# Square root on ACT and one Newton step for the reciprocal roots of the MLP and final norms, and POOL's squares of the second token half issued later

## The chip, the cores and the metric

The kernel runs on one core of one Trainium2 chip. The metric is the device time of one execution in microseconds (us), as the median of several executions. The core has five engines with instruction queues of their own: PE (matrix multiply), DVE (vector), ACT (scalar, functions from tables), POOL (a second elementwise engine) and SP (which issues DMAs). Each engine works its queue in order, and they wait for each other through semaphores.

## The reference, cut to what matters

A trunk of two layers on 1024 tokens of width 1024, in float32. Each layer mixes tokens (a gated MLP, a state space block and attention, side by side), then adds a squared-ReLU MLP; a last RMSNorm ends it. The change concerns three of the norms: that ahead of the MLP, in each of the two layers, and the last one.

```python
def rmsnorm(x, g):
    xf = x.astype(jnp.float32)
    var = jnp.mean(xf * xf, axis=-1, keepdims=True)
    return (xf * lax.rsqrt(var + EPS)).astype(x.dtype) * g
...
def squared_relu_mlp(h, w1, w2):
    return jnp.square(jax.nn.relu(h @ w1)) @ w2
...
        x = x + mix @ w_out[l]
        x = x + squared_relu_mlp(rmsnorm(x, norm_mlp_g[l]), mlp_w1[l], mlp_w2[l])
    return rmsnorm(x, final_norm_g)
```

## The kernel before, in words

Activations lie feature-major: `xt` is eight tiles of 128 features by 1024 tokens, and "half n" is 512 of the tokens. Each matrix product is done in three passes of a high and a low part (`whi`, `wlo`, `bhi`, `blo`), which ACT and DVE make (`split`: ACT casts, DVE subtracts). The products from `w_out` on are blocked as a seven-product scheme: a class `Run` walks through stages (`w_out`, then four times `w1` and `w2`), each of fourteen steps of 24 matmuls into `st` (line L998 in the profile). A stage's products are numbered p = 1 to 7, each in two steps (kh = 0 and 1). `hooks` maps (stage, step) to work that is put in behind that step.

A norm half goes like this. `after_mix` or `finish` squares each tile half on ACT (`sq<-x`) and adds the squares: the first four tiles on POOL, the others on DVE. `sq_rstd` lets PE sum over the features with eight small matmuls into `pss` (the tokens then lie on partitions, 128x4), and `rstd` forms the reciprocal root on DVE: the sum plus epsilon (`rv`), a first guess from the float's bits (`ry`, two integer operations), and three Newton steps of three operations (`rt`, `rt`, `ry`), twelve small operations in a row. PE then spreads `ry` over the partitions (`rb<-cs,ry`, eight small matmuls in the trace), ACT copies `rb` out of PSUM, and DVE forms the normed half `hB` (eight operations), which is split again for the next stage. In the last norm (`close_r`, `close_x`) the products go to `out` instead.

There are six such halves: in each layer half 0, whose `norm_r` and `norm_x` stand behind steps 10 and 11 of stage 0, and half 1, behind steps 0 and 1 of stage 1; and at the end half 1 (behind steps 10 and 11 of stage 8) and half 0 (`finish`, behind the last step). I call them A0 and B0 in layer 0, A1 and B1 in layer 1, and F and the tail. `rstd` serves other norms too (tags "n" and those of the attention), which the change leaves alone.

The order on each engine is not the order of the code: the tile framework schedules the instructions by a model of the engines, and `tc.high_priority()` lifts what is inside it ahead of other work. `L.zo` and `z_evac` belong to the start of layer 1: ACT empties the projection tiles `zps` with a Tanh, a copy and a small copy `dk`, and so frees their PSUM banks for later `zps` matmuls.

Of the kernel before, what the change touches and what calls it, by code (L numbers as in the profile page):

```python
# [9 lines left out]
F32 = mybir.dt.float32  # L10
F32R = mybir.dt.float32r
I32 = mybir.dt.int32
AF = mybir.ActivationFunctionType
ALU = mybir.AluOpType
# [4 lines left out]
P = 128  # L19
# [3 lines left out]
KD = D // P  # L23
DEPTH = 2
EPS = 1e-6
# [42 lines left out]
def trunk(ctx, tc, x, w_zdk, w_uv, w_f, w_q, w_kv, w_out, w1, w2, gains, pcol, prow, w_s, cst, out):  # L68
    nc = tc.nc

    const = ctx.enter_context(tc.tile_pool(name="const", bufs=1))
    rawp = ctx.enter_context(tc.tile_pool(name="raw", bufs=RAW))
    bigp = ctx.enter_context(tc.tile_pool(name="big", bufs=2))
    small = ctx.enter_context(tc.tile_pool(name="small", bufs=4))
# [4 lines left out]
    def G(dt=F32, name="g"):  # L79
        return gp.tile([P, 1024], dt, tag="g", name=name)  # L80

    def BIG(dt, name="big"):
        return bigp.tile([P, 8192], dt, tag="big", name=name)
# [3 lines left out]
    def bank(tag, name):  # L87
        return ps.tile([P, 512], F32, tag=tag, name=name, bufs=BANKS[tag])
# [5 lines left out]
    act = nc.scalar  # L94
    dve = nc.vector
    pool = nc.gpsimd
    pe = nc.tensor

    def tt(o, a, b, op, eng=None):
        (eng or dve).tensor_tensor(out=o, in0=a, in1=b, op=op)  # L100

    def stt(o, a, s, b, op0, op1):
        dve.scalar_tensor_tensor(out=o, in0=a, scalar=s, in1=b, op0=op0, op1=op1)

    def ts(o, a, s1, op0, s2=None, op1=None, eng=None):
        if op1 is None:
            (eng or dve).tensor_scalar(out=o, in0=a, scalar1=s1, scalar2=None, op0=op0)  # L107
        else:
            (eng or dve).tensor_scalar(out=o, in0=a, scalar1=s1, scalar2=s2, op0=op0, op1=op1)
# [8 lines left out]
    def mm(o, l, r, start, stop):  # L118
        pe.matmul(o, lhsT=l, rhs=r, start=start, stop=stop)  # L119

    def rstd(ss, n, tag):
        v = small.tile([P, n], F32, tag=tag + "v", name="rv")
        ts(v, ss, EPS, ALU.add)
        y = small.tile([P, n], F32, tag=tag + "y", name="ry")
        yi = y.bitcast(I32)
        ts(yi, v.bitcast(I32), 1, ALU.logical_shift_right)
        ts(yi, yi, -1, ALU.mult, MAGIC, ALU.add)
        t = small.tile([P, n], F32, tag=tag + "t", name="rt")
        for _ in range(3):
            tt(t, y, y, ALU.mult)  # L130
            stt(t, t, -0.5, v, ALU.mult, ALU.mult)
            stt(y, t, 1.5, y, ALU.add, ALU.mult)
        return y
# [12 lines left out]
    ones = const.tile([P, P], F32, name="ones")  # L146
    dve.memset(ones, 1.0)
    act.copy(maskq_r, ones)
    warm = bank("c", "warm")
    for _ in range(WARM):  # L150
        mm(warm[:, 0:P], ones, ones, True, True)
# [99 lines left out]
    def sq_rstd(acc, tag, t0=0, t1=NT, tg="c"):  # L251
        n = t1 - t0
        pss = bank(tg, "pss")
        for t in range(t0, t1):
            for i, q in enumerate(acc):
                mm(pss[:, t * 2:t * 2 + 2], q[:, t * P:(t + 1) * P], ones[:, 0:2], i == 0, i == len(acc) - 1)
        acc.clear()
        return rstd(pss[:, 2 * t0:2 * t1:2], n, tag)

    def hsl(h, k, a, b):  # L260
        return h[:, k * S + a:k * S + b]
# [55 lines left out]
    def z_rest(L):  # L317
        L.yb = [G(F32, "yb") for _ in range(3)]
        for n in range(4, NT):
            z_tile(L, n, PA("zps"))  # L320
            if n == 4:
                L.r = sq_rstd(L.sq, "n")
                ts(L.rh, L.r, 0.5, ALU.mult)
            if n == 5:
                for i in range(4):
                    z_evac(L, L.zo[i], L.zt[i])
            if n > 5:
                z_evac(L, L.zo[n - 2], L.zt[n - 2])
            if n == 5:
                prefetch(taken[0] + 2)  # L330
        for n in range(NT - 2, NT):
            z_evac(L, L.zo[n], L.zt[n])
        L.zo = L.wz = None
# [206 lines left out]
    def ssd_norm(L):  # L540
        yr = rstd(L.yss.rearrange("p c g -> p (c g)"), 16, "y").rearrange("p (c g) -> p c g", g=2)
        for j, segs in enumerate((((0, 128, 0),), ((0, 64, 0), (64, 128, 1)), ((0, 128, 1),))):
            v = L.yb[j].rearrange("p (c d) -> p c d", c=NT)
            for a, b, gq in segs:
                tt(v[:, :, a:b], v[:, :, a:b], yr[:, :, gq:gq + 1].broadcast_to([P, NT, b - a]), ALU.mult)

    def gmlp(L):
        vr = rstd(L.vss, NT, "v")
        for j in range(2):
            v = L.vv[j].rearrange("p (c d) -> p c d", c=NT)  # L550
            tt(v, v, vr.unsqueeze(2).broadcast_to([P, NT, P]), ALU.mult)
            tt(v, v, L.vg[:, j * P:(j + 1) * P].unsqueeze(1).broadcast_to([P, NT, P]), ALU.mult)
# [175 lines left out]
    def attention(L, l, xsrc):  # L728
# [140 lines left out]
        for _ in mixing:  # L869
            pass  # L870
        R = mlp(L, l, xsrc)
        R.prep(1)
        drain(2, VKEEP)
# [24 lines left out]
    def half(n):  # L898
        return slice(n * 512, n * 512 + 512)
# [150 lines left out]
    def sq_half(acc, xm, m, n, eng=None):  # L1050
        if m == 0 and acc:
            act.activation(acc[0][:, half(n)], xm[:, half(n)], AF.Square, scale=1.0 / 32.0)
            return
        sq = G(F32, "sq")
        act.activation(sq[:, half(n)], xm[:, half(n)], AF.Square, scale=1.0 / 32.0)  # L1055
        if m == 0:
            acc.append(sq)
        else:
            tt(acc[0][:, half(n)], acc[0][:, half(n)], sq[:, half(n)], ALU.add, eng)

    def half_bcast(r, o):
        for t in range(4):
            mm(o[:, t * P:(t + 1) * P], r[:, t:t + 1].broadcast_to([P, P]), ident, True, True)

    def mlp(L, l, xsrc):
# [3 lines left out]
        xt = [G(F32, "x") for _ in range(KD)]  # L1069
# [3 lines left out]
        acc, rs = {}, {}  # L1073
# [7 lines left out]
            return [mix[b * 4 + kh * 2 + kk][:, half(n)] for kk in range(2)]  # L1081

        def norm_r(n):
            rs[n] = sq_rstd(acc[n], "m", n * 4, n * 4 + 4, "a")

        def norm_x(n):
            if not hB:
                scr.clear()
                hB.append(BIG(F32, "hB").rearrange("p (k t) -> p k t", k=KD))
            o = bank("a", "rb")  # L1090
            half_bcast(rs.pop(n), o)
            rb = G(F32, "rb")
            act.copy(rb[:, 0:512], o)
            for m in range(KD):
                stt(hB[0][:, m, half(n)], xt[m][:, half(n)], gcol[:, 2 * l + 1, m:m + 1], rb[:, 0:512], ALU.mult, ALU.mult)

        def after_mix(p):
            if p == 3:
                acc[0] = []
                for m in range(4):  # L1100
                    sq_half(acc[0], xt[m], m, 0, pool)
            elif p == 7:
                for m in range(4, KD):
                    sq_half(acc[0], xt[m], m, 0)
            elif p == 2:
                acc[1] = []
                for m in range(4):
                    sq_half(acc[1], xt[m], m, 1, pool)
            elif p == 4:
                mix.clear()  # L1110
                for m in range(4, KD):
                    sq_half(acc[1], xt[m], m, 1)

        def to_next(p):
            if p == 2:
# [37 lines left out]
        def close_r(n):  # L1153
            rs[n] = sq_rstd(acc[n], "f", n * 4, n * 4 + 4, "a")
# [25 lines left out]
        class LazyB:  # L1180
            def __getitem__(self, k):
                return hB[0][k]

        stages = [Stage(w_out[l], mix_half, LATE1, add_to(xt, True, False, after_mix), True, False, scratch)]
        for q in range(NQ):
            end = q == NQ - 1
            stages.append(Stage(w1[l, q], halves_of(LazyB()), EARLY1 if q == 0 else LATE1, relu_to(Lazy())))
            stages.append(Stage(w2[l, q], halves_of(Lazy()), LATE1,
                                add_to(xt, False, not end, (finish if last else to_next) if end else None), chain=not end))
        hooks = {(0, 10): [lambda: norm_r(0)], (0, 11): [lambda: norm_x(0)],  # L1190
                 (1, 0): [lambda: norm_r(1)], (1, 1): [lambda: norm_x(1)]}
        if last:
            hooks[8, 10] = [lambda: close_r(1)]
            hooks[8, 11] = [lambda: close_x(1, 0)]
# [159 lines left out]
```

## Time and profile before

| | us |
|---|---|
| median of 3 runs (lowest, highest) | 2228.8 (2227.22, 2229.75) |
| the profiled execution, its own time | 2227.68 |
| its span, first to last instruction | 2225.8 |
| PE busy (share of the span) | 2180.0 (98%) |
| DVE busy | 1669.2 (75%) |
| ACT busy | 1131.5 (51%) |
| POOL busy | 470.9 (21%) |
| granted TensorE clock, mean | 0.992 |

The times are of single executions, the engine rows of one profiled execution; its time lies 1.1 us under the median. A share of busy time says how full an engine is, not how much shorter the kernel would be without a piece of its work: that is read at the place where the engine that sets the end waits. The granted clock is a share of TensorE's full 2.4 GHz; 0.5 is its lower level, 1.2 GHz.

### The profile page before, as it was taken

To read this page: it belongs to the slowest core of one execution; us is meant where nothing else is said; L and a number is where in the kernel's file an instruction comes from. 1 tells how busy PE (TensorE), PEld (TensorE's weight loads), DVE (VectorE), ACT (ScalarE), POOL (GpSimd) and SP (SyncE) were. 2 spreads that over 40 slices of the span, in tenths; PEclk is the share of its full clock that TensorE was granted. 3 is DMA by queue.
4 is the path that set the end of the run, shared out by engine and by line. 5 is a ranking of instruction groups with operands and counts; after the bars stand their busy time and mean duration, and the time that the engine had idled before them with its cause. 6 is when DMAs were issued, how large, how long until landed. Compare 5 with 4: busy or idle time off the path is not lost.

```text
span 2225.8 us, 28714 instructions
## 1 busy us (share of the span) xinstructions
PE 2180.0 (98%) x10844; PEld 1854.6 (83%) x10844; DVE 1669.2 (75%) x2516; ACT 1131.5 (51%) x1841; POOL 470.9 (21%) x444
## 2 busy tenths in 40 slices
PE   9999999999999999999999999999899999999996
PEld 8888989877888888888898888988788888888885
DVE  6788688788775876767847868878888767677576
ACT  6363577545445445355534626774464453543543
POOL 3152266121010001001301613751110010001011
PEclk9999999999999999999999999999999999999998
DMA  5211301354555546535412112023565465456532
GB/s 182 65 53 57 86 1 71 82 132 102 126 132 136 122 104 144 147 90 121 154 49 69 60 45 67 1 98 74 123 153 122 104 142 142 105 109 147 131 67 76
DMA packets 63625, 222.15 MB, mean 100 GB/s; under 512 B 7456, under 2 KB 7552, under 8 KB 63488
## 3 DMA queue, kind: packets, MB, share of 16 engines
q0 software_dynamic: 20736, 75.51, 19.6%
q1 hardware_dynamic: 42752, 144.83, 19.6%
q8 instruction: 85, 1.39, 0.2%
q14 instruction: 52, 0.43, 0.1%
HBM read 211.87 MB, written 8.44 MB: 99 GB/s over the span
## 4 chain that ended last, share of the span: by engine, by line
PE 94%; DVE 2%; issue 2%; ACT 1%; DMA 0%; POOL 0%; POOLq 0%; SPq 0%; ACTq 0%; DVEq 0%
PE st L998 61%; PE cqkv L119 5%; PE xbc L119 5%; PE uvps L119 4%; PE av L119 4%; PE sc L119 3%; PE zps L119 2%; PE pTp L789 2%; PE qps L119 2%; PE yps L119 1%; PE vps L119 1%; PE knps L119 1%; PE rb L119 1%; DVE mx L751 1%; DMA x<-in_x 0%
## 5 line engine op out<-in xcount | busy, mean ns | idle before, releaser
L998 PE MATMUL st<-blo,whi 128*128 128x512 f32 x2016 | 787.2, 390 | 0.0
L998 PE MATMUL st<-bhi,wlo 128*128 128x512 f32 x2016 | 786.6, 390 | 0.0
L998 PE MATMUL st<-bhi,whi 128*128 128x512 f32 x2016 | 781.4, 391 | 2.4 <-ACT bhi L115 2.4
L998 PEld LDWEIGHTS st<-bhi,whi 128*128 128x128 f32 x2016 | 380.5, 189 | 81.3 <-ACT bhi L115 2.7
L998 PEld LDWEIGHTS st<-bhi,wlo 128*128 128x128 f32 x2016 | 380.2, 189 | 79.1
L998 PEld LDWEIGHTS st<-blo,whi 128*128 128x128 f32 x2016 | 380.5, 189 | 78.3
L192 POOL DMA_DIRECT2D ssum<-in_w x96 | 84.2, 883 | 923.8 <-DVE wlo L100 380.5
L100 DVE TENSOR_TENSOR wlo<-raw,whi 128x1024 fp32r<-128x1024 f32 (+3 forms) x188 | 239.0, 1272 | 53.9 <-issue 29.8
L100 DVE TENSOR_TENSOR x<-x,st 128x512 f32<-128x512 f32 x296 | 196.0, 680 | 32.9 <-PE st L998 32.5
L115 ACT CAST bhi<-tsum 128x1024 fp32r<-128x1024 f32 x96 | 101.0, 1052 | 215.0 <-DVE tsum L100 173.9
L115 ACT CAST whi<-raw 128x1024 fp32r<-128x1024 f32 (+3 forms) x188 | 193.8, 1034 | 16.2 <-DVE blo L100 12.7
L107 POOL TENSOR_SCALAR p<-p,sm 128x1024 f32<-128x1024 f32 (+6 forms) x84 | 158.9, 1901 | 113.7 <-DVE sm L774 81.8
L115 ACT CAST whi<-ssum 128x1024 fp32r<-128x1024 f32 x108 | 113.5, 1051 | 112.2 <-PE st L998 57.1
L100 DVE TENSOR_TENSOR wlo<-ssum,whi 128x1024 fp32r<-128x1024 f32 x108 | 131.8, 1220 | 49.7 <-ACT whi L115 27.6
L100 DVE TENSOR_TENSOR blo<-tsum,bhi 128x1024 fp32r<-128x1024 f32 x96 | 117.3, 1222 | 46.4 <-ACT bhi L115 46.0
L119 PE MATMUL av<-pT,vhi 128*128 128x256 f32 x480 | 113.5, 298 | 0.8 <-DVE pT L100 0.5
L1043 ACT ACTIVATE hid<-hid 128x1024 f32<-128x1024 f32 x64 | 67.9, 1061 | 84.3 <-DVE hid L1036 84.0
L1036 DVE CUSTOM_DVE_ANT_0 hid<-st,hid 128x512 f32<-128x512 f32 x96 | 65.2, 686 | 56.8 <-PE st L998 56.5
L119 PE MATMUL sc<-B 96*128 96x384 f32 (+11 forms) x432 | 101.0, 351 | 3.1 <-ACT p L764 1.8
L100 POOL TENSOR_TENSOR sq<-sq 128x512 f32<-128x512 f32 (+1 forms) x37 | 60.7, 1647 | 191.9 <-ACT sq L1055 179.9
L100 DVE TENSOR_TENSOR blo<-hB,bhi 128x1024 fp32r<-128x1024 f32 x48 | 58.7, 1223 | 48.5 <-ACT bhi L115 48.5
L764 ACT ACTIVATE p<-sc,mx 128x512 f32<-128x512 f32 (+3 forms) x144 | 83.2, 583 | 21.0 <-DVE mx L100 14.2
(244 smaller groups left out, 3647.2 us busy)
## 6 DMA issues: line engine op xcount, KB each, us to landing
raw<-in_w SPq DMA_DIRECT2D x128, 512.0 KB, 3.7
ssum<-in_w POOLq DMA_DIRECT2D x96, 512.0 KB, 5.7
ssum<-in_w SPq DMA_DIRECT2D x32, 512.0 KB, 4.5
raw<-in_w POOLq DMA_DIRECT2D x32, 512.0 KB, 9.3
raw<-in_w_f SPq DMA_DIRECT2D x20, 512.0 KB, 3.5
x<-in_x SPq DMA_DIRECT2D x16, 512.0 KB, 6.9
raw<-in_w_out SPq DMA_DIRECT2D x16, 512.0 KB, 3.7
dec<-adr SPq DMA_DIRECT2D x16, 384.0 KB, 3.5
```

Source lines behind the costliest of these rows:

```text
L100: (eng or dve).tensor_tensor(out=o, in0=a, in1=b, op=op)
L107: (eng or dve).tensor_scalar(out=o, in0=a, scalar1=s1, scalar2=None, op0=op0)
L115: act.copy(hi, src)
L119: pe.matmul(o, lhsT=l, rhs=r, start=start, stop=stop)
L192: pool.dma_start(out=o, in_=src, accum_op=ALU.add)
L751: dve.reduce_max(mx[:, n:n + 1], on, axis=AX.X, negate=True)
L764: act.activation(pw[:, n * wh:(n + 1) * wh], os[n][:, :wh], AF.Exp, bias=mx[:, 0:1], accum_out=sm[:, n:n + 1])
L789: pe.transpose(pt[:, c0:c0 + P], pp[j][:, kt * P:(kt + 1) * P], ident)
L998: pe.matmul(os[j], lhsT=w[:, cw], rhs=b[:, cb], start=first and n == 0, stop=last and n == 2, skip_group_check=True)
L1036: dve._custom_dve(TENSOR_ADD_SAT, out=d, in0=os[j], in1=d, s0=0.0 if full[0] else BIGGEST, s1=-BIGGEST if full[0] else 0.0)
L1043: act.activation(d, d, AF.Square)
```

## The change

`sq_rstd` calls a new function for the tags "m" (the norm ahead of the MLP) and "f" (the last norm). It takes the square root on ACT with epsilon as a bias tile, the reciprocal on DVE, and one Newton step instead of three. `norm_r`, the broadcast of `norm_x`, and the squares of tiles 4 to 7 are put under `tc.high_priority()`. The squares of tiles 0 to 3 of half 1, with POOL's additions, leave `after_mix` (p = 2) and go behind step 12 of stage 0, after `norm_x(0)`. In `finish` the squares stay where they were.

```diff
+    def rstd_act(ss, n, tag):
+        v = small.tile([P, n], F32, tag=tag + "v", name="rv")
+        y = small.tile([P, n], F32, tag=tag + "y", name="ry")
+        t = small.tile([P, n], F32, tag=tag + "t", name="rt")
+        act.activation(t, ss, AF.Sqrt, bias=eps)
+        ts(v, ss, EPS, ALU.add)
+        dve.reciprocal(y, t)
+        tt(t, y, y, ALU.mult)
+        stt(t, t, -0.5, v, ALU.mult, ALU.mult)
+        stt(y, t, 1.5, y, ALU.add, ALU.mult)
+        return y
...
+    eps = const.tile([P, 1], F32, name="eps")
+    dve.memset(eps, EPS)
...
-        return rstd(pss[:, 2 * t0:2 * t1:2], n, tag)
+        return (rstd_act if tag in ("m", "f") else rstd)(pss[:, 2 * t0:2 * t1:2], n, tag)
...
         def norm_r(n):
-            rs[n] = sq_rstd(acc[n], "m", n * 4, n * 4 + 4, "a")
+            with tc.high_priority():
+                rs[n] = sq_rstd(acc[n], "m", n * 4, n * 4 + 4, "a")
...
-            o = bank("a", "rb")
-            half_bcast(rs.pop(n), o)
-            rb = G(F32, "rb")
-            act.copy(rb[:, 0:512], o)
+            with tc.high_priority():
+                o = bank("a", "rb")
+                half_bcast(rs.pop(n), o)
+                rb = G(F32, "rb")
+                act.copy(rb[:, 0:512], o)
...
             elif p == 7:
-                for m in range(4, KD):
-                    sq_half(acc[0], xt[m], m, 0)
-            elif p == 2:
-                acc[1] = []
-                for m in range(4):
-                    sq_half(acc[1], xt[m], m, 1, pool)
+                with tc.high_priority():
+                    for m in range(4, KD):
+                        sq_half(acc[0], xt[m], m, 0)
             elif p == 4:
                 mix.clear()
-                for m in range(4, KD):
-                    sq_half(acc[1], xt[m], m, 1)
+                with tc.high_priority():
+                    for m in range(4, KD):
+                        sq_half(acc[1], xt[m], m, 1)
+
+        def squares():
+            acc[1] = []
+            for m in range(4):
+                sq_half(acc[1], xt[m], m, 1, pool)
...
+                 (0, 12): [squares], (1, 0): [lambda: norm_r(1)], (1, 1): [lambda: norm_x(1)]}
```

What the scheduler makes of it, at three places of layer 0. On DVE at A0, from the sum of the squares on, before the change (`x<-x,st` adds the products of the step that ends here to `xt`; one more Newton operation pair and `hB` x8 follow):

```order
L107 TENSOR_SCALAR rv<-pss 128x4
L100 TENSOR_TENSOR x<-x,st 128x512
L107 TENSOR_SCALAR ry<-rv 128x4
L109 TENSOR_SCALAR ry<-ry 128x4
L100 TENSOR_TENSOR rt<-ry 128x4
L100 TENSOR_TENSOR x<-x,st 128x512
L103 SCALAR_TENSOR_TENSOR rt<-rt,rv 128x4
L103 SCALAR_TENSOR_TENSOR ry<-rt,ry 128x4
L100 TENSOR_TENSOR rt<-ry 128x4
L103 SCALAR_TENSOR_TENSOR rt<-rt,rv 128x4
L103 SCALAR_TENSOR_TENSOR ry<-rt,ry 128x4
L100 TENSOR_TENSOR rt<-ry 128x4
```

The same place with the change:

```order
L107 TENSOR_SCALAR rv<-pss 128x4
L127 RECIPROCAL ry<-rt 128x4
L100 TENSOR_TENSOR x<-x,st 128x512
L100 TENSOR_TENSOR rt<-ry 128x4
L103 SCALAR_TENSOR_TENSOR rt<-rt,rv 128x4
L103 SCALAR_TENSOR_TENSOR ry<-rt,ry 128x4
L100 TENSOR_TENSOR x<-x,st 128x512
L103 SCALAR_TENSOR_TENSOR hB<-x,gcol,rb 128x512 x8
```

Twelve small operations have become five, and only one of the two additions to `x` is left between them. In the built program `rv` and, through it, the reciprocal wait for ACT's square root.

On ACT at A0 before the change, from the casts ahead of it to the casts for stage 1:

```order
L115 CAST bhi<-scr 128x1024
L1055 ACTIVATE sq<-x 128x512 x4
L1093 COPY rb<-rb 128x512
L115 CAST whi<-raw 128x1024
L115 CAST bhi<-hB 128x1024
L115 CAST whi<-raw 128x1024
L115 CAST bhi<-hB 128x1024
L1055 ACTIVATE sq<-x 128x512 x4
```

With the change:

```order
L115 CAST bhi<-scr 128x1024
L125 ACT_TABLE_LOAD
L125 ACTIVATE rt<-pss,eps 128x4
L1109 COPY rb<-rb 128x512
L115 CAST whi<-raw 128x1024
L115 CAST bhi<-hB 128x1024
L1069 ACTIVATE sq<-x 128x512 x4
L115 CAST whi<-raw 128x1024
L115 CAST bhi<-hB 128x1024
L1069 ACTIVATE sq<-x 128x512 x4
```

A load of a function table (which waits for nothing) and the square root have come in, and the four squares of half 1 have moved from ahead of the copy of `rb` to behind the first cast of `hB`. The whole program has four such loads where it had one: at its start, here, at the same place of layer 1, and ahead of the first Tanh of `z_evac` of layer 1, where the waits of the Tanh stand ahead of the load.

On POOL before the change, from the end of layer 0's attention to the first loads of stage 1 (`ssum` and `raw` rows are DMAs that add a second block of weights):

```order
L107 TENSOR_SCALAR p<-p,sm 128x1024
L192 DMA ssum<-in_w_out 128x1024 x4
L100 TENSOR_TENSOR sq<-sq 128x512 x6
L192 DMA ssum<-in_w 128x1024 x2
L192 DMA raw<-in_w 128x1024 x2
```

With the change:

```order
L107 TENSOR_SCALAR p<-p,sm 128x1024
L206 DMA ssum<-in_w_out 128x1024 x4
L100 TENSOR_TENSOR sq<-sq 128x512 x3
L206 DMA ssum<-in_w 128x1024
L100 TENSOR_TENSOR sq<-sq 128x512 x3
L206 DMA ssum<-in_w 128x1024
L206 DMA raw<-in_w 128x1024 x2
```

The three additions of half 1 now stand behind one DMA and ahead of the other; layer 1 is the same in this. Nearly all other rows of the program stand as they did.

## Rows read from the trace of the kernel before

**Rows 1.** Waits of PE, longest first: total us, times, longest.
```profile
PE rb L119 <- DVE ry L103: 20.1, 6, 4.6
PE st L998 <- ACT bhi L115: 2.4, 2, 1.2
```
**Rows 2.** Timeline of PE: start, length, idle before it at A0, B0 and F.
```profile
475.76 2.08 PE L119 MATMUL rb<-cs,ry 128*128 128x128 f32 x8 [4.55 <-DVE ry L103]
...
504.77 1.27 PE L119 MATMUL rb<-cs,ry 128*128 128x128 f32 x8 [2.43 <-DVE ry L103]
...
2194.89 1.76 PE L119 MATMUL rb<-cs,ry 128*128 128x128 f32 x8 [3.70 <-DVE ry L103]
```
**Rows 3.** Windows, PE alone: stretch, its length, PE busy, granted clock, DMA share, GB/s.
```profile
475.76:482.00 6.24, 6.24 (x19) 0.52 0.88 150
504.77:510.00 5.23, 5.23 (x20) 0.67 0.00 0
1571.10:1576.00 4.90, 4.90 (x20) 0.70 0.84 139
1598.64:1606.00 7.36, 7.36 (x24) 0.58 0.01 2
2194.89:2200.00 5.11, 5.11 (x19) 0.67 0.22 79
394.29:398.00 3.71, 3.71 (x17) 1.00 0.47 141
```
**Rows 4.** Timelines of DVE, POOL and ACT at A0.
```profile
469.04 0.16 DVE L107 TENSOR_SCALAR rv<-pss 128x4 f32<-128x4 f32 x1
469.86 0.69 DVE L100 TENSOR_TENSOR x<-x,st 128x512 f32<-128x512 f32 x1 [0.66 <-PE st L998]
...
471.45 1.18 DVE L100 TENSOR_TENSOR rt<-ry 128x4 f32<-128x4 f32 x1
...
471.35 1.26 POOL L100 TENSOR_TENSOR sq<-sq 128x512 f32<-128x512 f32 x1 [0.17 <-ACT sq L1055]
...
464.81 1.04 ACT L115 CAST bhi<-scr 128x1024 fp32r<-128x1024 f32 x1
```
**Rows 5.** Timeline of DVE ahead of B0 and in it.
```profile
499.07 1.23 DVE L100 TENSOR_TENSOR blo<-hB,bhi 128x1024 fp32r<-128x1024 f32 x1 [1.47 <-ACT bhi L115]
502.37 0.16 DVE L107 TENSOR_SCALAR rv<-pss 128x4 f32<-128x4 f32 x1 [2.08 <-PE pss L119]
...
504.55 0.16 DVE L103 SCALAR_TENSOR_TENSOR ry<-rt,ry 128x4 f32<-128x4 f32 x1
```
**Rows 6.** Groups by line and form: count, busy us, mean ns.
```profile
L148 ACT ACT_TABLE_LOAD x1 | 1.3, 1283 | 0.7 <-PEq L1346 0.7
L358 ACT ACTIVATE dk<-zps,ry 128x38 f32<-128x38 f32 x16 | 5.6, 352 | 0.0
...
L409 DVE RECIPROCAL sp_r<-sp_r 128x48 f32<-128x48 f32 x2 | 0.9, 453 | 0.1
...
L103 DVE SCALAR_TENSOR_TENSOR hB<-x,gcol,rb 128x512 f32<-128x512 f32 x32 | 21.6, 746 | 10.5 <-ACT rb L1093 10.5
```
**Rows 7.** Timeline of DVE under POOL's additions, at the end of layer 0.
```profile
1097.39 1.71 DVE L103 SCALAR_TENSOR_TENSOR hTlo<-x,gcol,hThi 128x512 fp32r<-128x512 f32 x1 [0.77 <-ACT hThi L240]
```
**Rows 8.** Timelines of DVE and PE: first low part of `hB`, and its use.
```profile
484.99 1.22 DVE L100 TENSOR_TENSOR blo<-hB,bhi 128x1024 fp32r<-128x1024 f32 x1
...
491.41 0.39 PE L998 MATMUL st<-blo,whi 128*128 128x512 f32 x1
```
**Rows 9.** Timelines of ACT and PE: first tile emptied in layer 1, and the next use of its bank.
```profile
1134.34 0.29 ACT L358 ACTIVATE dk<-zps,ry 128x38 f32<-128x38 f32 x1
...
1135.96 0.44 PE L119 MATMUL zps<-whi,hThi 128*128 128x422 f32 x1
```
**Rows 10.** Timeline of ACT at the program's start.
```profile
0.73 1.28 ACT L148 ACT_TABLE_LOAD   x1 [0.73 <-PEq L1346]
2.02 0.30 ACT L148 CAST maskq_r<-ones 128x128 fp32r<-128x128 f32 x1
```

More of the change, by code (lines that the diff above doesn't have):

```diff
@@ L1190, in mlp @@
         hooks = {(0, 10): [lambda: norm_r(0)], (0, 11): [lambda: norm_x(0)],
-                 (1, 0): [lambda: norm_r(1)], (1, 1): [lambda: norm_x(1)]}
+                 (0, 12): [squares], (1, 0): [lambda: norm_r(1)], (1, 1): [lambda: norm_x(1)]}
         if last:
```

## Prediction

> **What bounds the kernel now.** The page's busy times come first: PE is busy for 98% of the span, the next engine, DVE, for 75%. So only a stretch in which PE stands still, or runs at its lower clock, can be taken back. The list of PE's waits says where these are: PE waits 20.1 us in six pieces for the last small operation of a reciprocal root (`ry`) before it can spread it as `rb`; no other wait is over 2.4 us in total [rows 1]. These six are the halves that the change touches. In the timeline of PE each is one row: 4.55 us at A0 (A1 is the same to the hundredth), 2.43 at B0 (B1 and the tail are the same), 3.70 at F [rows 2]. The reader is to see in the windows that each wait is paid twice: after it the granted clock is at its lower level, 1.2 GHz, for some microseconds. The loss in a window is its length times what is missing in the clock [rows 3]: A0 6.24 x 0.48 = 3.0, B0 5.23 x 0.33 = 1.7, A1 4.90 x 0.30 = 1.5, B1 7.36 x 0.42 = 3.1, F 5.11 x 0.33 = 1.7, in all 11.0 us. A wait of 1.2 us (half of the 2.4 in two pieces) ahead of 394.29 was followed by a clock of 1.00 [rows 1, 3].
>
> Why 4.55 at A0, when the same twelve operations cost 2.43 at B0? At B0 DVE runs them alone, one every 0.198 us (502.37 to 504.55, eleven steps) [rows 5]. At A0 additions to `x` lie between them, and some take six times their length: `rt`, at 471.45 for 1.18 us, ends with the POOL addition that runs from 471.35 for 1.26 us, while the addition that reads PSUM, at 469.86, keeps its 0.69 us [rows 4]. So a DVE operation with SBUF operands alone is held while POOL adds. These POOL additions are the squares of half 1, which nobody needs until B0: the ones that the change moves.
>
> **The change part by part.** *The new chain.* It is a square root, `rv`, the reciprocal and three operations of a Newton step. No row shows a Sqrt. It cannot be shorter than the 0.16 us of a DVE operation of that shape [rows 5]; the nearest ACT row, the small copy `dk` out of PSUM (128x38), has 0.352 [rows 6]. I take 0.3, nearer to that row. The reciprocal lies between the same 0.16 and 0.453 for twelve times the columns [rows 6]; I take 0.17. So the chain is 0.33 with the hand-over, plus four steps of 0.198, plus 0.16: 1.3 us after the sums, against 2.35 before. Bounds: 1.15 and 1.65.
>
> *A0 and A1.* The sums are there at 469.04. Square root to 469.37, `rv` and reciprocal to 469.75, the addition to `x` from 469.86 to 470.55 [rows 4], three small ones to 471.15, undisturbed, since the squares of half 1 no longer stand there. PE is free at 475.76 - 4.55 = 471.21 [rows 2], so almost the whole wait goes: 4.5, and with it the slow clock. A0 gains 4.5 + 3.0 = 7.5, A1 4.5 + 1.5 = 6.0. The operations behind the waiting reciprocal on DVE, the additions to `x`, wait for PE anyway.
>
> *The table loads.* The profile has one load of 1283 ns [rows 6]; the change adds three. Those of A0 and A1 wait for nothing and follow the cast that ends at 465.85 [rows 4]: done at 467.13, 1.9 us before the sums, so they cost nothing; without that cover each would add 1.28. The third stands behind the waits of the first Tanh of layer 1 and so delays the emptying of the first tile from 1134.63 to 1135.91. PE uses the bank at 1135.96 [rows 9]. Cost 0, by a hair. The load at the start was followed by a cast of ordinary length 0.01 us after its end [rows 10]. The Trainium skill, "ScalarE: Activation LUTs", section "What ACT_TABLE_LOAD costs", speaks against the change: a switch costs the 1283 ns and a drain of about 1380 ns more, 2.66 us in all, and calls are to be batched by table set. By it the loads at A0 and A1 would still be hidden, and the third would not.
>
> *The moved squares.* ACT squares them behind the first cast of `hB`, so POOL's three additions fall upon DVE's eight `hB` operations, all SBUF alone. Under POOL's additions at the end of layer 0 an operation of this kind took 1.71 us [rows 7] against 0.746 for `hB` [rows 6], so one addition costs DVE 0 to 1.26 us; by that row about 1.0, three 2.9. Who waits for that? First the low part of `hB`, which step 0 of stage 1 needs: it was done at 486.21 and used at 491.41 [rows 8], 5.2 us later. About 2.2 of these were the slow clock (the 3.0 less what `rb` itself lost, some 0.8), so 3.0 remain: just covered. Then the sums of half 1: DVE stood idle for 1.47 and 2.08 us ahead of B0 [rows 5]. PE now comes some 2.2 earlier against DVE and the additions take 2.9, together 1.5 more than that idle time; some of the rest shrinks with it, as DVE's additions to `x` no longer wait. I take 0.6 us per layer as lost at B0 and B1 for this and for operands of the next steps, to which PE comes sooner; bounds 0 and 1.5. The POOL DMA behind the additions is late by their length, for weights that are cast after B0.
>
> *B0 and B1.* The chain is 1.05 us shorter, less 0.6: 0.45. PE's wait becomes about 2.0, and less where DVE is in time. Does the clock then stay up? 1.2 us kept it, 2.43 did not [rows 1 to 3]; 2.0 lies between. At B0 the fall came late: `rb` still took 1.27 us there, against 2.08 at A0 [rows 2]. So at 2.43 it was lost only partly, and I take it that at 2.0 and less it stays: 1.7 and 3.1. So 2.15 and 3.55; with the bounds 0 to 2.75 and 0 to 4.15.
>
> *F and the tail.* At F the squares stay, so POOL can still hold one of the small operations. Ending as at A0 the chain leaves at most 0.3 of the 3.70; held once by 1.26, some 1.5. I take 2.8 gained, and the 1.7 of the clock: 4.5 (3.9 to 5.1). The tail is latency from the sums to the last store: 1.05.
>
> The sum: 7.5 + 6.0 + 4.5 + 2.15 + 3.55 + 1.05 = 24.75. Against the profiled execution's 2227.68 that is 2202.9; this execution lies 1.1 under the median, so I forecast 2204.
>
> **The rivals.** (1) *The clock falls at B0 and B1 all the same.* Their gain is then 0.45 each in place of 2.15 and 3.55, 4.8 less: 2208.8. For it: the new waits lie between a length that kept the clock and one that lost it. Against it: they should be nearer to the shorter where DVE is in time. Chance 0.22. (2) *The moved squares become the new wait.* If each addition holds DVE for its whole 1.26 us, 3.8 in a layer, the low part of `hB` is 0.8 late, and the sums of half 1 come 2.4 late; B0 and B1 gain nothing, and each layer loses about 0.8: 24.75 - 5.7 - 1.6 = 17.4, 2211.4. For it: the rt row at A0 was held to POOL's very end. Against: the 1.71 row. Chance 0.12. (3) *The switch is longer than its row.* If it holds ACT for the load's 1.28 us once more, the first tile of layer 1 is empty at 1137.19, 1.2 after PE wants the bank: 2205.2. Against it: the cast right behind the load at the start. Chance 0.1. It is what the page of the Trainium skill named above would make of this place. (4) *Slower than before.* The mechanism would be that of (2) at a higher price: POOL's additions hold DVE between the copy of `rb` and the first low part of `hB`, PE stands still, and the clock falls behind that too. With 3.0 of slack and some 3 us of clock, a layer loses 12.4, half of the gain, when the three additions cost DVE 12.4 us, 4.1 each. At the 1.26 that an addition lasts this is out of reach; at 6 each the time would be 2228.8 - 24.75 + 2 x 18 = 2240. Chance 0.03. (5) *The change does not do what it says*: DVE, in order, waits for a late square root, and the six waits keep their length: 2228.8. At A0 ACT would have to start the root 4.5 us after the sums, at B0 1.05; but no ACT work is queued ahead of it that PE had not released before the sums. Chance 0.02.
>
> **How the numbers follow.** My forecast has 0.51: 2204, with 2202 to 2207 as its own range (the bounds of B0, B1 and F are together 1.8 better; the longer chain of 1.65 at B0, B1 and the tail, no gain beside the clock at B0 and B1, and F held, are some 2.5 worse). Cases (1) and (3) lie inside 2200.5 to 2210.5; (2) partly above. So the range is 2200.5 to 2210.5. About 0.2%, 4.5 us, is what a measurement of this kernel can tell from no change. Faster: 0.51 + 0.22 + 0.12 + 0.1 = 0.95; same: 0.02; slower: 0.03.
>
> **What would show it.** In the profile after: the six waits of `rb` for `ry` shrink from 20.1 to some 6 us, near 0 at A0 and A1; the granted clock in the windows behind A0, A1 and F is 1.00; the POOL additions of half 1 lie beside `hB`; ACT has four table loads, none ahead of a wait of PE. I am wrong if PE waits for `blo` or `hB` in stage 1, if the windows behind B0 and B1 still show a clock of 0.6, or if `zps` waits for `dk` in layer 1.

## The result and the profile after

The changed kernel takes 2203.72 us (median; 2202.99 to 2203.73), the kernel before 2228.16 beside it. The ratio is 0.9889, with a 95% interval of 0.9872 to 0.9906. The profiled execution has a span of 2201.9 us, against 2225.8.

First the waits of PE, as the profile sums them (total us, times, longest):

```profile
PE rb L119 <- DVE ry L103: 4.9, 4, 1.7
PE st L1012 <- ACT bhi L115: 2.4, 2, 1.2
```

The six waits of `rb` have shrunk from 20.1 us to 4.9; the next kind of wait is what it was [rows 1]. So 15.2 of the 23.9 us were standing time. To place the rest, take one row that both programs have at each of the six halves: the sums over the features, `pss`. In the kernel before (timeline of PE; start, length):

```profile
468.06 0.95 PE L119 MATMUL pss<-ones,sq 128*128 128x2 f32 x8
...
501.39 0.95 PE L119 MATMUL pss<-ones,sq 128*128 128x2 f32 x8
...
1563.39 0.95 PE L119 MATMUL pss<-ones,sq 128*128 128x2 f32 x8
...
1595.26 0.95 PE L119 MATMUL pss<-ones,sq 128*128 128x2 f32 x8
...
2187.80 0.95 PE L119 MATMUL pss<-ones,sq 128*128 128x2 f32 x8
...
2210.76 1.05 PE L119 MATMUL pss<-ones,sq 128*128 128x2 f32 x8 [2.18 <-DVE sq L100]
```

The same rows after, with the spread `rb` behind each and, first, a wait at the start of stage `w_out` of layer 0:

```profile
394.37 2.07 PE L1012 MATMUL st<-bhi,whi 128*128 128x512 f32 x4 [1.19 <-ACT bhi L115]
...
469.65 0.95 PE L119 MATMUL pss<-ones,sq 128*128 128x2 f32 x8
472.66 1.16 PE L119 MATMUL rb<-cs,ry 128*128 128x128 f32 x8
...
495.49 0.95 PE L119 MATMUL pss<-ones,sq 128*128 128x2 f32 x8
498.12 1.16 PE L119 MATMUL rb<-cs,ry 128*128 128x128 f32 x8 [1.69 <-DVE ry L103]
...
1555.44 0.95 PE L119 MATMUL pss<-ones,sq 128*128 128x2 f32 x8
1558.45 1.16 PE L119 MATMUL rb<-cs,ry 128*128 128x128 f32 x8
...
1581.28 0.95 PE L119 MATMUL pss<-ones,sq 128*128 128x2 f32 x8
1583.92 1.16 PE L119 MATMUL rb<-cs,ry 128*128 128x128 f32 x8 [1.69 <-DVE ry L103]
...
2170.41 0.95 PE L119 MATMUL pss<-ones,sq 128*128 128x2 f32 x8
2174.05 1.16 PE L119 MATMUL rb<-cs,ry 128*128 128x128 f32 x8 [0.26 <-DVE ry L103]
...
2188.32 1.05 PE L119 MATMUL pss<-ones,sq 128*128 128x2 f32 x8 [2.18 <-DVE sq L100]
2190.60 2.08 PE L119 MATMUL rb<-cs,ry 128*128 128x128 f32 x8 [1.23 <-DVE ry L103]
```

A stretch runs from one `pss` to the next, the last from `pss` to the span's end:

| stretch | before, us | after, us | gained | forecast |
|---|---|---|---|---|
| start to A0 | 468.06 | 469.65 | -1.59 | 0 |
| A0 | 33.33 | 25.84 | 7.49 | 7.5 |
| B0, to layer 1's A1 | 1062.00 | 1059.95 | 2.05 | 2.15 |
| A1 | 31.87 | 25.84 | 6.03 | 6.0 |
| B1, to F | 592.54 | 589.13 | 3.41 | 3.55 |
| F | 22.96 | 17.91 | 5.05 | 4.5 |
| tail | 15.04 | 13.58 | 1.46 | 1.05 |
| sum | 2225.8 | 2201.9 | 23.90 | 24.75 |

The windows of PE behind its waits (stretch, length, PE busy, granted clock, DMA share, GB/s) show the other share, the clock:

```profile
394.37:399.37 5.00, 5.00 (x16) 0.67 0.50 120
472.66:477.66 5.00, 5.00 (x27) 1.00 0.65 150
498.12:503.12 5.00, 5.00 (x26) 1.00 0.61 184
...
2174.05:2179.05 5.00, 5.00 (x26) 1.00 0.18 71
```

Behind A0, B0 and F (A1 and B1 alike) the clock is at its full 2.4 GHz, where before it fell to 1.2 GHz for some microseconds [rows 3]. The first row is the one loss: the wait of 1.19 us at 394 stood in the kernel before too and kept the clock there [rows 3]; here the window lacks 5.00 x 0.33 = 1.65 us, and the way from this row to A0 is 1.51 us longer than before. Nothing in the program differs ahead of it except a small constant at the start. Of the ten kernels that were profiled in all, which are alike up to there, three lost the clock at this wait; what decides it is not known.

The rows of `rb` split each stretch in two (before the change they start at 475.76, 504.77, 1571.10, 1598.64, 2194.89 [rows 2, 3] and 2214.25). Ahead of `rb`, where the wait lies, A0, B0, A1, B1, F and the tail gained 4.69, 0.75, 4.70, 0.74, 3.45 and 1.21 us. Behind it, where the clock counts, they gained 2.80, 1.30, 1.33, 2.67, 1.60 and 0.25.

At A0 itself (timelines of ACT, DVE, POOL and PE):

```profile
467.49 1.28 ACT L125 ACT_TABLE_LOAD   x1
470.64 0.26 ACT L125 ACTIVATE rt<-pss,eps 128x4 f32<-128x4 f32 x1 [1.86 <-PE pss L119]
...
471.01 0.17 DVE L127 RECIPROCAL ry<-rt 128x4 f32<-128x4 f32 x1
...
472.45 0.16 DVE L103 SCALAR_TENSOR_TENSOR ry<-rt,ry 128x4 f32<-128x4 f32 x1
...
479.78 1.62 POOL L100 TENSOR_TENSOR sq<-sq 128x512 f32<-128x512 f32 x1
481.48 1.62 POOL L100 TENSOR_TENSOR sq<-sq 128x512 f32<-128x512 f32 x1
...
480.17 1.78 DVE L103 SCALAR_TENSOR_TENSOR hB<-x,gcol,rb 128x512 f32<-128x512 f32 x1
481.88 2.31 DVE L100 TENSOR_TENSOR wlo<-raw,whi 128x1024 fp32r<-128x1024 f32 x1
484.11 1.21 DVE L100 TENSOR_TENSOR blo<-hB,bhi 128x1024 fp32r<-128x1024 f32 x1
...
485.49 0.40 PE L1012 MATMUL st<-blo,whi 128*128 128x512 f32 x1
```

The table load ends 1.87 us before the sums come. The chain is over at 472.61, while PE still works on the step ahead of `rb`. The moved POOL additions now hold DVE elsewhere: an `hB` of 1.78 us where the mean before the change was 0.746 [rows 6], a `wlo` of 2.31 where the subtraction behind it, of the same shape, takes 1.21. The first low part of `hB` is done at 485.32, and PE takes it at 485.49, with 0.17 us to spare.

The third new table load, at the start of layer 1 (ACT and PE):

```profile
1125.42 1.28 ACT L370 ACT_TABLE_LOAD   x1 [24.77 <-DVE rh L107]
...
1127.66 0.30 ACT L372 ACTIVATE dk<-zps,ry 128x38 f32<-128x38 f32 x1
...
1128.01 0.46 PE L119 MATMUL zps<-whi,hThi 128*128 128x422 f32 x1
```

It delays the emptying of the first tile to 1127.96; PE needs the bank at 1128.01 and has no idle time there. So 0.05 us were left.

At B0 (DVE, ACT):

```profile
496.10 1.22 DVE L100 TENSOR_TENSOR blo<-hB,bhi 128x1024 fp32r<-128x1024 f32 x1
497.24 0.16 DVE L107 TENSOR_SCALAR rv<-pss 128x4 f32<-128x4 f32 x1
...
496.47 0.26 ACT L125 ACTIVATE rt<-pss,eps 128x4 f32<-128x4 f32 x1
```

The root is done at 496.73, but DVE is still at a subtraction and starts `rv` only at 497.24.

### The profile page after: what moved, and what is told of

Read it like the earlier page. It is cut to its first block, busy times and chain, and to the rows that moved or that the text cites. A ratio compares the mean times of both kernels' runs of the same rounds, so it can differ in the third digit from the quotient of the medians.

```text
span 2201.9 us, 28671 instructions
## 1 busy us (share of the span) xinstructions
PE 2172.1 (99%) x10844; PEld 1847.5 (84%) x10844; DVE 1661.2 (75%) x2475; ACT 1136.9 (52%) x1850; POOL 472.7 (21%) x444
## 3 DMA queue, kind: packets, MB, share of 16 engines
q0 software_dynamic: 20736, 75.51, 20.1%
## 4 chain that ended last, share of the span: by engine, by line
PE 93%; DVE 3%; issue 2%; ACT 1%; DMA 0%; POOL 0%; POOLq 0%; SPq 0%; ACTq 0%; DVEq 0%
PE st L1012 60%; PE cqkv L119 5%; PE xbc L119 5%; PE uvps L119 4%; PE av L119 4%; PE sc L119 3%; PE zps L119 2%; PE pTp L803 2%; PE qps L119 2%; PE yps L119 1%; PE vps L119 1%; PE knps L119 1%; DVE hB L103 1%; DVE mx L765 1%; PE rb L119 1%
```

## The experiments

Eight kernels ran, each timed in several rounds beside the kernel before (2227.46 us for the first four, 2227.69 for the others).

**The order without the root** (`order_only`).

```diff
-        return (rstd_act if tag in ("m", "f") else rstd)(pss[:, 2 * t0:2 * t1:2], n, tag)
+        return rstd(pss[:, 2 * t0:2 * t1:2], n, tag)
```

> The changed order without the new root: the three Newton steps on DVE as before, but POOL's squares of half 1 beside hB. My theory (DVE's small operations at A0 were held by POOL): undisturbed, twelve operations and two additions to x take about 3.7 us there, so the wait of rb at A0 and A1 falls from 4.55 to some 1.8; B0, B1 stay at 2.43 with the slow clock behind them, F at 3.70, the tail at 2.43: about 2220 us (2224 if the clock falls at A0 and A1 too). Rival (the length of the chain alone made the waits, POOL had no part): A0 and A1 keep 4.55, about 2228 us.

2221.2 us, ratio 0.997 (0.9958 to 0.9981): about 6.3 us gained. PE at A0:

```profile
473.51 1.33 PE L119 MATMUL rb<-cs,ry 128*128 128x128 f32 x8 [2.23 <-DVE ry L103]
```

The same twelve operations as before, but without POOL beside them, leave PE waiting 2.23 us where it had waited 4.55 [rows 2] (2.22 at A1). The expected wait was 1.8, and the clock fell behind this one (0.66 in 5 us). DVE and POOL in the kernel before, then DVE here:

```profile
470.46 0.75 DVE L107 TENSOR_SCALAR ry<-rv 128x4 int32<-128x4 int32 x1
...
469.89 1.29 POOL L100 TENSOR_TENSOR sq<-sq 128x512 f32<-128x512 f32 x1 [18.55 <-ACT sq L1055]
...
470.54 0.16 DVE L107 TENSOR_SCALAR ry<-rv 128x4 int32<-128x4 int32 x1
```

DVE has the same operations in the same order at this place in both kernels, the two additions to `x` included, so the new priorities did not change it. Before the change three small operations were held, each to the end of a POOL addition (0.75, 1.18 [rows 4] and, at 474.12, 1.19 us); here every one takes 0.15 to 0.17. The rival, that POOL had no part, is out.

**The root without the order** (`chain_only`).

```diff
+            elif p == 2:
+                acc[1] = []
+                for m in range(4):
+                    sq_half(acc[1], xt[m], m, 1, pool)
...
-        def squares():
-            acc[1] = []
-            for m in range(4):
-                sq_half(acc[1], xt[m], m, 1, pool)
...
-                 (0, 12): [squares], (1, 0): [lambda: norm_r(1)], (1, 1): [lambda: norm_x(1)]}
+                 (1, 0): [lambda: norm_r(1)], (1, 1): [lambda: norm_x(1)]}
```

The squares of tiles 4 to 7 lose their high priority as well.

> The new root without the changed order: POOL's squares of half 1 at their old place, beside the chain of A0. My theory: one POOL addition still holds one of the three small operations at A0 and A1, so a wait of 0.5 to 1.0 us stands there where the changed kernel has none; the clock stays at 1.00; hB is not held any more. Some 2 us worse than the changed kernel: about 2205.5 us. Rival (the move is what keeps the clock): waits of 1.5 to 2.5 us at A0 and A1 and the lower clock behind them, about 2212 us.

2206.29 us, ratio 0.9903 (0.9890 to 0.9917): 21.2 us gained. DVE, POOL and PE at A0:

```profile
470.62 1.04 DVE L100 TENSOR_TENSOR rt<-ry 128x4 f32<-128x4 f32 x1
...
471.90 1.11 DVE L103 SCALAR_TENSOR_TENSOR ry<-rt,ry 128x4 f32<-128x4 f32 x1
...
470.35 2.64 POOL L100 TENSOR_TENSOR sq<-sq 128x512 f32<-128x512 f32 x2 [18.86 <-ACT sq L1069]
...
473.06 1.16 PE L119 MATMUL rb<-cs,ry 128*128 128x128 f32 x8 [1.70 <-DVE ry L103]
```

Two of the three small operations, not one, are held, each until a POOL addition ends, and PE waits 1.70 us at A0 and A1. The clock stays at 1.00 there, so the move is not what keeps it. At B0 and B1 the wait is 1.22 and 1.23, against 1.69 with the move: there the move costs 0.47. Twice (1.70 - 0.47) is 2.5 us. In the two profiles the stretches A0 and A1 are 1.80 us longer each without the move, B0 and B1 0.52 and 0.50 shorter, 2.6 in all. The medians differ by 2.6 too, but `chain_only` ranges from 2204.05 to 2208.2, so the rows are the better evidence. The move alone and the root alone would add up to 27.5; together they gave about 24, since both take time from the same waits at A0 and A1.

**Two Newton steps** (`newton2`): the three lines of the step stand twice.

> The changed kernel with two Newton steps in place of one: three more DVE operations, 0.6 us, at each of the six places. Waits of rb: about 0.5 at A0 and A1, 2.3 at B0 and B1, 0.9 at F, 1.8 in the tail. If the length of the wait decides on the clock (2.43 lost it before the change, 1.69 kept it after), 2.3 loses it at B0 and B1: about 2212 us. If not the length but something else at these places decided, the clock stays 1.00: about 2207 us.

2214.39 us, ratio 0.9938 (0.9925 to 0.9952). B0 and B1 wait 2.27 and 2.28 us, and the clock in the 5 us behind them is 0.66. A0 and A1 wait 1.25 us, not the expected 0.5: DVE puts a second addition to `x` between the small operations. F came out otherwise than expected (DVE, POOL, PE):

```profile
2181.17 1.21 DVE L103 SCALAR_TENSOR_TENSOR ry<-rt,ry 128x4 f32<-128x4 f32 x1
...
2181.10 1.26 POOL L100 TENSOR_TENSOR sq<-sq 128x512 f32<-128x512 f32 x1 [0.18 <-ACT sq L1072]
...
2182.43 1.98 PE L119 MATMUL rb<-cs,ry 128*128 128x128 f32 x8 [2.93 <-DVE ry L103]
```

Three operations of 0.2 us lengthen this wait from 0.26 to 2.93: the chain no longer ends before POOL's third addition begins, its last operation is held until that ends, and an addition to `x` slips in as well. The clock falls behind it too.

**Two Newton steps, and F's squares put off** (`newton2_late`): as the change does it in each layer.

```diff
-            elif p == 2:
-                acc[0] = []
-                for m in range(4):
-                    sq_half(acc[0], xt[m], m, 0, pool)
...
+        def late_squares():
+            acc[0] = []
+            for m in range(4):
+                sq_half(acc[0], xt[m], m, 0, pool)
...
+            hooks[8, 12] = [late_squares]
```

> Two Newton steps, and at F the squares of tiles 0 to 3 put off behind step 12 of stage 8, as the change does it in each layer. At F three more operations had cost 2.67 us, not 0.6, and the last of them ended with a POOL addition. If POOL held it, the wait at F falls from 2.93 to some 0.5 and the clock stays 1.00 behind it: 2.4 + 1.7 = 4.1 better than two Newton steps alone, 2210.3 us. If DVE's own additions to x make that wait, it stays above 2 us and the time at 2214.

2213.36 us, ratio 0.9934 (0.9922 to 0.9947). The wait at F falls to 1.25 us (0.5 was expected; an addition to `x` still lies between the small operations) and the clock behind it stays at 1.00, so POOL had held it, as `newton2` showed in its rows. But the time moves by about 1 us, not 4:

```profile
2196.59 1.05 PE L119 MATMUL pss<-ones,sq 128*128 128x2 f32 x8 [3.56 <-DVE sq L100]
```

The squares put off are late for the sums of the tail: that wait grows from 2.18 to 3.56 us. F gives 1.7 us of waiting and 1.7 of clock, the tail takes 1.4 back: 2.0, and the profiled spans differ by 1.7 (2212.4 and 2210.7).

**No Newton step** (`newton0`), the reciprocal of the square root used as it is.

> The changed kernel with no Newton step: the reciprocal of ACT's square root is used as it is, so the root is less exact. Three DVE operations and rv less: 0.6 us off the waits at B0 and B1 (1.69 to 1.1), 0.26 at F (to 0), 0.6 in the tail: about 2 us better than the changed kernel, 2201.6 us. If DVE comes late for other reasons (a cast's subtraction stands ahead of the reciprocal at B0) the gain is still there, since the three operations stand behind it. Rival (what PE waits for at B0 is by now the next operand, not the root): no gain at B0 and B1, 2202.9 us.

2200.34 us, ratio 0.9878 (0.9864 to 0.9891): better than the changed kernel by some 3 us (2198.81 to 2202.71 against 2202.99 to 2203.73). B0 and B1 wait 1.03, F nothing, the tail 0.57, as expected: the three operations less are gained at each of these places, and the rival is out. Windows behind B0 and B1:

```profile
495.76:500.76 5.00, 5.00 (x19) 0.66 0.69 224
...
1582.22:1587.22 5.00, 5.00 (x26) 1.00 0.70 228
```

The same wait of 1.03 us lost the clock at one and kept it at the other.

**No Newton step, squares at their old place** (`newton0_old`): `chain_only` with the shorter chain.

> No Newton step (so a less exact root), and POOL's squares of half 1 at their old place. If the move paid only because POOL held the small operations of the chain, it is not needed here: one reciprocal on DVE is left to hold, and at A0 it is done some 1.2 us before PE is free. At B0 and B1 DVE stands idle when the sums come (1.96 us in the run with the new root alone), so the wait falls from 1.03 to about 0.5 at each: 1 us better than no Newton step with the move, 2199.3 us. Rival (the move is worth its 2 us by itself, through the order it gives ACT and POOL): 2202 us or more.

2199.88 us, ratio 0.9874 (0.9860 to 0.9887). At A0 and A1 PE does not wait, at B0 and B1 0.57 us in place of 1.03. By the rows the move is then not needed; the times of the two (2198.81 to 2202.71 and 2198.62 to 2200.65) overlap too much to show the 0.9 us. Both beat the changed kernel, at the price of the less exact root.

**Three POOL additions more** (`pool_six`), on data that nobody reads.

```diff
+            junk = G(F32, "sq")
+            for _ in range(3):
+                tt(junk[:, half(0)], xt[0][:, half(1)], xt[1][:, half(1)], ALU.add, pool)
```

> The changed kernel with three further POOL additions in each layer, on data that nobody uses, beside hB: six where the change has three. The three cost DVE's eight hB operations 1.5 us together, and the first low part of hB came 0.17 us before PE used it. If each further addition costs DVE the same 0.5 us, PE waits for that low part by about 1.3 us in each layer, without a fall of the clock: 2206.5 us. If each holds DVE for its whole length, about 1.3 to 1.6 us, the wait is some 4 us in each layer and the clock falls behind it: about 2215 us.

2214.12 us, ratio 0.9939 (0.9926 to 0.9951): 10.4 us more than the changed kernel. PE in layer 0:

```profile
487.92 0.50 PE L1012 MATMUL st<-blo,whi 128*128 128x512 f32 x1 [2.05 <-DVE blo L100]
...
501.75 2.07 PE L119 MATMUL rb<-cs,ry 128*128 128x128 f32 x8 [2.77 <-DVE ry L103]
```

The spare 0.17 is gone: PE waits 2.05 us for the low part (2.29 in layer 1), then 2.77 at B0, where ACT and DVE had fallen behind: the root started 0.9 us after the sums, and `rv` stood behind two subtractions. The clock was 0.50 in the 5 us after that. My 0.5 us for an addition was wrong: I had spread 1.5 us over three from the `hB` group alone, while the third had held the `wlo` behind it. From `rb` to the first low part it is 14.99 us here and 12.66 in the changed kernel, for two additions more (the sixth had to wait for that low part itself): 2.33 us, about 1.2 each.

**Two table loads on the path** (`table_f`): a Tanh of `pss` into `ry`, which is overwritten, ahead of the square root at F and in the tail.

> The changed kernel with a Tanh (its result is overwritten) ahead of the square root at F and in the tail, so that ACT loads two tables at each. In the tail the first load lies beside the wait for the sums, the Tanh and the second load stand on the path: by the load's 1.28 us and an operation of 0.26 the tail is 1.6 longer. At F both loads are on the path, 2.9 us, and the clock falls behind: 1.6 + 2.9 + 1.7, about 2210 us. If a switch costs ACT twice its row, the tail is 4.3 longer and F 5.5, about 2215 us, and the rows show idle time behind each load.

2211.3 us, ratio 0.9924 (0.9906 to 0.9942). ACT in the tail:

```profile
2195.61 0.17 ACT L126 ACTIVATE ry<-pss 128x4 f32<-128x4 f32 x1 [0.58 <-PE pss L119]
2195.79 1.28 ACT L127 ACT_TABLE_LOAD   x1
2197.09 0.26 ACT L127 ACTIVATE rt<-pss,eps 128x4 f32<-128x4 f32 x1
```

The Tanh takes 0.17, the load 1.28, and the square root starts 0.02 after it; PE's wait in the tail grows from 1.23 to 2.70, by 1.47, the sum of the three. So on the path too a switch costs its row and nothing more. At F the wait is 3.74 instead of 0.26, more than the two loads and the Tanh (2.73): the later chain runs beside POOL's additions, and two of its small operations take 1.11 and 1.12 us.

## Why the prediction was right, point by point

- **Two prices for each wait, its length and the clock behind it.** Shown by the table and the windows: A0 gained 7.49 us, 4.69 ahead of `rb` and 2.80 behind it. The second price was taken too high at every place: the missing clock in the windows had given 3.0, 1.7, 1.5, 3.1 and 1.7 at A0, B0, A1, B1 and F, 11.0 in all, and the stretches behind `rb` gained 9.7. At B0 and B1 the gain ahead of `rb` (0.75 and 0.74 for the forecast 0.45) made most of that good, so the close agreement of these two lines of the table is in part luck.
- **POOL's additions held the chain at A0.** Shown by `order_only`, which moves them and leaves the chain and DVE's order alone, and by the rows of `chain_only` and `newton2`. The share was 2.3 us of the 4.55; the length of the chain made the rest.
- **The new chain's price.** Square root 0.26 (taken: 0.3), reciprocal 0.17 (0.17). Where nothing holds DVE, the wait falls from 2.43 to 1.22 (B0 of `chain_only`; 1.23 in the tail), so the chain is 1.2 us shorter, not 1.05. At B0 with the move DVE's lag behind a subtraction leaves 1.69, a fall of 0.74: the lag cost 0.47, where I had put 0.6.
- **The moved squares, about 1.0 us of DVE for each addition, just covered.** The rows say 1.0 to 1.1 each, and the cover was 0.17 us. `pool_six` shows what stood behind it: rival 2's mechanism, and the way to rival 4, need only a few more such additions; with the three of the change nobody waits, and the root comes in time, so rivals 2, 4 and 5 did not happen.
- **The table loads cost nothing.** Right at all three places. Rival 3 is out by the rows of the load and by `table_f`. The Trainium skill, "ScalarE: Activation LUTs", section "What ACT_TABLE_LOAD costs", adds a drain of about 1.38 us to the same 1.28. No run here shows it, and 1.47 us on the path in the tail leaves no room for it.
- **The clock stays at B0 and B1.** Right, with waits of 1.69; `newton2` shows rival 1 at 2.27, where it is lost. That I set the line between the two was a choice, and it came out; part of it was luck, since `newton0` lost the clock at B0 behind a wait of only 1.03.
- **F and the tail were sized too low**, by 0.55 and 0.41 us: at F POOL held one operation, but for 0.4 us only, and the wait fell by 3.44 instead of 2.8; in the tail the chain was 1.2 us shorter instead of 1.05, and some 0.25 came behind `rb`.
- **What the sum did not have**: the 1.59 us before A0, of which 1.51 lie behind the wait at 394, where the clock fell. It more than offset the two low terms (0.96): the sum gave 2202.9 for the profiled execution, which took 2203.73. The 1.1 us that I added to come to a median had no counterpart after the change, where the profiled execution lies at the median. So it is luck that 2204 and 2203.72 lie so close. Without the 1.59 this execution would have come to about 2202.1, still inside the forecast's own range.

## What to carry to other kernels

A wait of the engine that sets the end is best priced twice, as its length and as the clock that follows it, both from the same place of the trace. When small operations in a row take longer at one place than at another, look which engine runs beside the long ones; shortening the chain and moving the neighbour then pay for the same microseconds, so their gains do not add. Work that is moved off a path lands beside something: count the slack there (here 0.17 us was left, and in the tail 1.4 us came back).

## What the runs showed of the hardware that was not expected

- The clock after a wait is not set by the wait's length alone. In the ten profiled executions, the tail apart (little runs behind it), every wait of 2.22 us or more ahead of `rb` was followed by 5 us at a clock of 0.50 to 0.71. Waits of 1.70 or less ahead of `rb` kept 1.00, except once (1.03, at B0 of `newton0`). But the unchanged wait of 1.19 at 394 lost it in three of the ten, and the waits of 2.05 and 2.29 for the low part in `pool_six` kept it. What else decides was not settled.
- DVE's and POOL's operations with operands in SBUF take turns: a POOL addition, 1.26 us at F, takes 1.62 beside `hB`, and the `hB` beside it 1.78 for 0.746. The Trainium skill, "SBUF — State Buffer", section "Who interferes with whom", says that a DVE instruction with two SBUF inputs contends with an instruction of GpSimd (POOL) that reads SBUF, and calls the contention an exclusive lock. The rows of `chain_only` agree: operations of 0.16 us took 1.04 and 1.11, each to the end of the addition.
